# A column mean over 8192 rows: six 32 KB buffers used as a chain and then as a ring, instead of two pairs and a single

## Chip, core, metric

One core of one Trainium2 chip. The metric is the device time of one execution in microseconds; several executions are timed and medians quoted. The profile's span is about 2 us shorter than the time; where I take a time line apart, I use the span. Buffers are given per partition: 32 KB is one row group, 128 rows of 8192 fp32 values, 4.194 MB over all partitions.

## The reference

```python
def setup_inputs():
    return {"x": np.random.randn(8192, 8192).astype(np.float32)}

def reference(x):
    return np.mean(x, axis=0)
```

268.4 MB are read, and 32 KB are written.

## The kernel before

Row groups arrive by DMA. VectorE adds each into `acc`; at the end TensorE multiplies by a block of 1/8192 to sum over the partitions, with the last rows going to TensorE partly without a VectorE add. Five row groups of landing room (two pairs, one single) and `acc` make six buffers of 32 KB.

```python
pairs = [sb.tile([P, 2, N], f32, name=f"pair{i}") for i in range(2)]
single = sb.tile([P, N], f32, name="single")
acc = sb.tile([P, N], f32, name="acc")
...
def load(dst, src):
    queue = nc.sync if g < 30 else nc.scalar       # two DMA queues, one after the other
    queue.dma_start(out=dst, in_=src)
...
while g < G - 5:                                   # pair, pair, single, pair, pair, single ...
    if k % 3 < 2:
        t = pairs[i]
        load(t[:], rows(g, 2).rearrange("(p j) c -> p j c", j=2))
        ...                                        # the first pair makes acc
            add(t[:, 0, :], 0, N)                  # acc += first row group
            add(t[:, 1, :], 0, N)                  # acc += second row group
    else:
        load(single[:], rows(g))
        add(single, 0, N)
...
plan = [                                           # order of the closing matmuls, 512 columns each
    (r61, 0, 5), (r62, 8, 15), (acc, 8, 15), (r63, 0, 8), (acc, 0, 8), (acc, 15, 16),
    (r63, 8, 12), (r63, 12, 15), (r63, 15, 16),
]
...
# outputs: banks 0 and 1 on SyncE's queue, bank 2 and bank 3 on ScalarE's, edge on SyncE's
```

Of the kernel before, what the change touches and what calls it, by code (L numbers as in the profile page):

```python
# [1 line left out]

# [4 lines left out]


@with_exitstack
def kernel(  # L10
    ctx: ExitStack,
    tc: tile.TileContext,
    x: bass.AP,
    out: bass.AP,
):













    nc = tc.nc
    f32 = mybir.dt.float32  # L30
    M, N = x.shape
    P = nc.NUM_PARTITIONS
    F = 512
    W = F // 4
    NBLK = N // F - 1
    G = M // P

    sb = ctx.enter_context(tc.tile_pool(name="sb", bufs=1))
    psp = ctx.enter_context(tc.tile_pool(name="psum", bufs=1, space=bass.MemoryType.PSUM))

    pairs = [sb.tile([P, 2, N], f32, name=f"pair{i}") for i in range(2)]
    single = sb.tile([P, N], f32, name="single")
    acc = sb.tile([P, N], f32, name="acc")
    ones = sb.tile([P, 32], f32, name="ones")
    warm = sb.tile([P, 32], f32, name="warm")
    nc.gpsimd.memset(ones[:], 1.0 / M)  # L46
    nc.scalar.copy(out=warm[:], in_=ones[:])  # L47
    banks = [psp.tile([P, F], f32, name=f"bank{b}") for b in range(4)]
    edge = psp.tile([P, W], f32, name="edge")

    def add(row, lo, hi):
        nc.vector.tensor_add(out=acc[:, lo:hi], in0=acc[:, lo:hi], in1=row[:, lo:hi])  # L52

    def load(dst, src):
        queue = nc.sync if g < 30 else nc.scalar
        queue.dma_start(out=dst, in_=src)  # L56

    def rows(g, n=1):
        return x[g * P:(g + n) * P, :]

    g = 0
    k = 0
    np_ = 0
    while g < G - 5:
        if k % 3 < 2:
            i = np_ % 2
            np_ += 1
            t = pairs[i]
            load(t[:], rows(g, 2).rearrange("(p j) c -> p j c", j=2))
            if g == 0:  # L70
                nc.vector.tensor_add(out=acc[:], in0=t[:, 0, :], in1=t[:, 1, :])  # L71
            else:
                add(t[:, 0, :], 0, N)
                add(t[:, 1, :], 0, N)
            g += 2
        else:
            load(single[:], rows(g))
            add(single, 0, N)
            g += 1
        k += 1  # L80

    pa, pb = pairs[np_ % 2], pairs[(np_ + 1) % 2]
    r59, r60, r61, r62, r63 = single, pa[:, 0, :], pa[:, 1, :], pb[:, 0, :], pb[:, 1, :]
    load(r59[:], rows(g))
    add(r59, 0, N)
    load(r60, rows(g + 1))
    add(r60, 0, N)
    load(r61, rows(g + 2))
    add(r61, 5 * F, N)
    for lo, hi in [(0, 8), (8, 16)]:  # L90
        load(r62[:, lo * F:hi * F], rows(g + 3)[:, lo * F:hi * F])
    add(r62, 0, 8 * F)
    add(r62, NBLK * F, N)
    for lo, hi in [(0, 8), (8, 12), (12, 15), (15, 16)]:
        load(r63[:, lo * F:hi * F], rows(g + 4)[:, lo * F:hi * F])

    plan = [
        (r61, 0, 5),
        (r62, 8, 15),
        (acc, 8, 15),  # L100
        (r63, 0, 8),
        (acc, 0, 8),
        (acc, 15, 16),
        (r63, 8, 12),
        (r63, 12, 15),
        (r63, 15, 16),
    ]
    left = [sum(lo <= i < hi for _, lo, hi in plan) for i in range(NBLK + 1)]
    full = list(left)
    for row, lo, hi in plan:  # L110
        for i in range(lo, hi):
            for q in range(4) if i == NBLK else [i % 4]:
                c = i * F + (q * W if i == NBLK else 0)
                dst = edge if i == NBLK else banks[i // 4]
                tc.keep_in_program_order(nc.tensor.matmul(  # L115
                    out=dst[32 * q:32 * q + 32, :],
                    lhsT=ones[:],
                    rhs=row[:, c:c + (W if i == NBLK else F)],
                    start=left[i] == full[i],
                    stop=left[i] == 1,  # L120
                    tile_position=(0, 32 * q),
                    skip_group_check=True,
                ))
            left[i] -= 1

    res01 = sb.tile([P, 2, F], f32, name="res01")
    res2 = sb.tile([P, F], f32, name="res2")
    res3 = sb.tile([P, F], f32, name="res3")
    resedge = sb.tile([P, W], f32, name="resedge")
    nc.scalar.copy(out=res01[:, 0, :], in_=banks[0][:])  # L130
    nc.scalar.copy(out=res01[:, 1, :], in_=banks[1][:])  # L131
    nc.vector.tensor_copy(out=res2[:], in_=banks[2][:])  # L132
    tc.keep_in_program_order(nc.scalar.copy(out=res3[:96, :], in_=banks[3][:96, :]))  # L133
    nc.vector.tensor_copy(out=resedge[:], in_=edge[:])  # L134
    nc.sync.dma_start(
        out=out[0:8 * F].rearrange("(b q c) -> q b c", b=2, q=4), in_=res01[0:P:32, :, :])
    tc.keep_in_program_order(nc.scalar.dma_start(
        out=out[8 * F:12 * F].rearrange("(q c) -> q c", q=4), in_=res2[0:P:32, :]))
    tc.keep_in_program_order(nc.scalar.dma_start(
        out=out[12 * F:15 * F].rearrange("(q c) -> q c", q=3), in_=res3[0:96:32, :]))  # L140
    tc.keep_in_program_order(nc.sync.dma_start(
        out=out[15 * F:].rearrange("(q c) -> q c", q=4), in_=resedge[0:P:32, :]))


# [1 line left out]
_INS = ['x']  # L146
_OUTS = [((8192,), 'float32')]


# [23 lines left out]
```

## Time and profile before

| | before |
|---|---|
| time, median of 4 runs | 631.94 us (631.73 to 632.30) |
| span of the profiled run | 629.3 us |
| DMA engines, a full window | 433 GB/s, share 1.00 |
| VectorE | 533.6 us, 85% |
| last load landed (landing records of the trace) | 624.0 us |

The row to read first is that of the DMA engines, since it is full. The lines, and what follows from them, are in the prediction below.

### The profile page before, as it was taken

The page shows a single profiled execution, that of the slowest core. Times are in us where ns is not written, and L with a number is a line of the kernel's source. Part 1 is how long each engine was busy: PE and PEld are TensorE (multiplying, and loading weights), DVE is VectorE, ACT ScalarE, POOL GpSimd, SP SyncE. Part 2 cuts the span into 40 slices and gives each one's busy share as a digit, 9 for nine tenths or more (in the row PEclk, how much of TensorE's full clock was granted, in tenths as well). Part 3 has the DMA queues.
Part 4 walks back from the last instruction along what each step waited for, and adds up shares of the span by engine and source line. Part 5 has one row for each costly group of instructions (what it writes and reads, how often), then busy time and mean ns, then how long its engine had stood idle before and what let it go on. Part 6 is the DMA issues. An engine that isn't in the chain of part 4 may idle for free.

```text
span 629.3 us, 444 instructions
## 1 busy us (share of the span) xinstructions
PE 14.9 (2%) x100; PEld 4.9 (1%) x100; DVE 533.6 (85%) x65; ACT 3.3 (1%) x5; POOL 0.3 (0%) x5
## 2 busy tenths in 40 slices
PE   0000000000000000000000000000000000000027
PEld 0000000000000000000000000000000000000002
DVE  0539889889889889899499999888988988988995
ACT  0000000000000000000000000000000000000001
POOL 0000000000000000000000000000000000000000
PEclk9999999999999999999999999999999999999998
DMA  9999999999999999999999999999999999999995
GB/s 400 408 429 442 454 406 460 408 433 442 450 408 458 417 425 437 454 408 450 421 454 412 454 412 454 413 454 412 454 412 454 412 454 412 454 412 427 431 426 238
DMA packets 6371, 268.48 MB, mean 427 GB/s; under 512 B 719, under 2 KB 723, under 8 KB 994
## 3 DMA queue, kind: packets, MB, share of 16 engines
q10 hardware_dynamic: 3758, 142.62, 52.5%
q1 hardware_dynamic: 2612, 125.85, 46.3%
q14 instruction: 1, 0.01, 0.0%
HBM read 268.44 MB, written 0.03 MB: 427 GB/s over the span
## 4 chain that ended last, share of the span: by engine, by line
DMA 63%; DVE 35%; PE 2%; issue 0%; ACT 0%; SPq 0%; ACTq 0%; DVEq 0%
DMA pair<-in_x_dram 55%; DVE acc L52 35%; DMA single<-in_x_dram 8%; PE bank L115 2%; ACT res L133 0%; SPq L56 0%; PE edge L115 0%; ACTq L56 0%; DVEq L52 0%
## 5 line engine op out<-in xcount | busy, mean ns | idle before, releaser
L52 DVE TENSOR_TENSOR acc<-acc,pair 128x8192 f32<-128x8192 f32 (+3 forms) x50 | 419.6, 8393 | 56.5 <-DMA pair<-in_x_dram 55.5
L52 DVE TENSOR_TENSOR acc<-acc,single 128x8192 f32<-128x8192 f32 x12 | 104.3, 8692 | 9.4 <-DMA single<-in_x_dram 9.1
L71 DVE TENSOR_TENSOR acc<-pair 128x8192 f32<-128x8192 f32 x1 | 8.7, 8691 | 22.7 <-DMA pair<-in_x_dram 22.7
L115 PE MATMUL bank<-pair,ones 128*32 128x512 f32 x54 | 11.9, 800 | 610.7 <-DMA pair<-in_x_dram 610.7
L115 PEld LDWEIGHTS bank<-pair,ones 128*32 128x32 f32 x54 | 2.6, 128 | 616.4 <-issue 616.1
L115 PE MATMUL bank<-acc,ones 128*32 128x512 f32 x30 | 6.2, 661 | 0.0
L130 ACT COPY res<-bank 128x512 f32<-128x512 f32 x1 | 0.6, 587 | 620.3 <-DMA pair<-in_x_dram 620.3
L132 DVE COPY res<-bank 128x512 f32<-128x512 f32 x1 | 0.7, 692 | 3.2 <-PE bank L115 3.2
L115 PEld LDWEIGHTS bank<-acc,ones 128*32 128x32 f32 x30 | 1.7, 125 | 2.9 <-issue 2.5
L47 ACT ACT_TABLE_LOAD x1 | 1.3, 1283 | 0.7 <-PEq L157 0.7
L115 PE MATMUL edge<-pair,ones 128*32 128x128 f32 x8 | 0.8, 276 | 0.0
L115 PE MATMUL edge<-acc,ones 128*32 128x128 f32 x8 | 0.8, 272 | 0.0
L134 DVE COPY resedge<-edge 128x128 f32<-128x128 f32 x1 | 0.3, 291 | 0.4 <-PE bank L115 0.4
L133 ACT COPY res<-bank 96x512 f32<-96x512 f32 x1 | 0.6, 582 | 1.3 <-PE bank L115 1.3
L131 ACT COPY res<-bank 128x512 f32<-128x512 f32 x1 | 0.6, 586 | 0.3 <-PE bank L115 0.3
L115 PEld LDWEIGHTS edge<-acc,ones 128*32 128x32 f32 x8 | 0.5, 110 | 0.5 <-issue 0.3
L115 PEld LDWEIGHTS edge<-pair,ones 128*32 128x32 f32 x8 | 0.4, 109 | 0.6 <-issue 0.6
L47 ACT COPY warm<-ones 128x32 f32<-128x32 f32 x1 | 0.2, 217 | 0.0
L46 POOL MEMSET ones<- 128x32 f32 x1 | 0.1, 125 | 0.3 <-POOLq L157 0.3
L157 POOL MEMSET const-bfloat16-1.0<- 128x1 bf16 x1 | 0.1, 102 | 0.0
L157 POOL MEMSET const-uint8-127<- 128x1 uint8 x1 | 0.1, 102 | 0.0
L157 POOL MEMSET const-float32-0.0<- 128x1 f32 x1 | 0.1, 99 | 0.2 <-issue 0.2
(1 smaller groups left out, 0.1 us busy)
## 6 DMA issues: line engine op xcount, KB each, us to landing
single<-in_x_dram SPq DMA_DIRECT2D x6, 4096.0 KB, 40.3
single<-in_x_dram ACTq DMA_DIRECT2D x6, 4096.0 KB, 31.9
pair<-in_x_dram ACTq DMA_DIRECT2D x2, 4096.0 KB
pair<-in_x_dram ACTq DMA_DIRECT2D x3, 2048.0 KB, 26.3
pair<-in_x_dram ACTq DMA_DIRECT2D x1, 1024.0 KB, 28.4
pair<-in_x_dram ACTq DMA_DIRECT2D x1, 768.0 KB, 29.8
pair<-in_x_dram ACTq DMA_DIRECT2D x1, 256.0 KB, 29.9
pair<-in_x_dram SPq DMA_DIRECT2D x12, 30.9
```

The costliest lines, as they stand in the source:

```text
L46: nc.gpsimd.memset(ones[:], 1.0 / M)
L47: nc.scalar.copy(out=warm[:], in_=ones[:])
L52: nc.vector.tensor_add(out=acc[:, lo:hi], in0=acc[:, lo:hi], in1=row[:, lo:hi])
L71: nc.vector.tensor_add(out=acc[:], in0=t[:, 0, :], in1=t[:, 1, :])
L115: tc.keep_in_program_order(nc.tensor.matmul(out=dst[32 * q:32 * q + 32, :], lhsT=ones[:], rhs=row[:, c:c + (W if i == NBLK else F)], start ...
L130: nc.scalar.copy(out=res01[:, 0, :], in_=banks[0][:])
L131: nc.scalar.copy(out=res01[:, 1, :], in_=banks[1][:])
L132: nc.vector.tensor_copy(out=res2[:], in_=banks[2][:])
L133: tc.keep_in_program_order(nc.scalar.copy(out=res3[:96, :], in_=banks[3][:96, :]))
L134: nc.vector.tensor_copy(out=resedge[:], in_=edge[:])
L157: nc = _bacc.Bacc("TRN2", target_bir_lowering=False, num_devices=1)
```

## The change

It was meant to let nearly all loads be pairs, to halve the number of VectorE instructions in the opening, to have VectorE wait for one thing at a time, and to leave TensorE less to do after the last load, with fewer output transfers in each other's way. Cut to its core:

```diff
+    bufs = sb.tile([P, U, N], f32, name="bufs")     # U = 6
+    acc = bufs[:, U - 1, :]
-        queue = nc.sync if g < 30 else nc.scalar
+        queue = nc.sync if g < 30 and g != 2 else nc.scalar
+    def add(dst, src, dma=None, own=True):
+        ins = nc.vector.tensor_add(out=dst, in0=dst, in1=src).ins
+        ...
+        if dma and own:      # a GpSimd nop waits for load and previous add, VectorE for the nop
+        ...
+    while g < CHAIN:                                 # CHAIN = 12 row groups
+        u = g % U
+        dmas.append(load_pair(u, u + 1))
+        ...                                          # v: the pair of buffers before u
+            add(bufs[:, u:u + 2, :], bufs[:, v:v + 2, :], dmas[-1])   # 16384 columns
+        g += 2
+    add(acc, bufs[:, U - 2, :])
+    while g < G - 8:                                 # ring of five
+        dma = load_pair((g - CHAIN) % (U - 1), (g + 1 - CHAIN) % (U - 1))
+        add(buf(g + 1), buf(g), dma, own=False)
+        add(acc, buf(g + 1))
+        g += 2
+    ...                                              # five single rows, then r61, r62, r63
     plan = [
         (r61, 0, 5),
+        (acc, 8, 15),
         (r62, 8, 15),
-        (acc, 8, 15),
-        (r63, 0, 8),
         (acc, 0, 8),
         (acc, 15, 16),
+        (r63, 0, 8),
...
+    # outputs: banks 0 to 2 in one transfer, then bank 3, on SyncE's queue; edge on ScalarE's
```

More of the change, by code (lines that the diff above doesn't have):

```diff
@@ L36 @@
     G = M // P
+    U = 6
+    CHAIN = 12
+    sync = mybir.DependencyInfo(mybir.DependencyClass.Sync, mybir.DependencyReason.DATA)
     sb = ctx.enter_context(tc.tile_pool(name="sb", bufs=1))
     psp = ctx.enter_context(tc.tile_pool(name="psum", bufs=1, space=bass.MemoryType.PSUM))
-    pairs = [sb.tile([P, 2, N], f32, name=f"pair{i}") for i in range(2)]
-    single = sb.tile([P, N], f32, name="single")
-    acc = sb.tile([P, N], f32, name="acc")
+    bufs = sb.tile([P, U, N], f32, name="bufs")
+    acc = bufs[:, U - 1, :]
     ones = sb.tile([P, 32], f32, name="ones")
@@ L49 @@
     edge = psp.tile([P, W], f32, name="edge")
-    def add(row, lo, hi):
-        nc.vector.tensor_add(out=acc[:, lo:hi], in0=acc[:, lo:hi], in1=row[:, lo:hi])
     def load(dst, src):
-        queue = nc.sync if g < 30 else nc.scalar
-        queue.dma_start(out=dst, in_=src)
+        queue = nc.sync if g < 30 and g != 2 else nc.scalar
+        ins = queue.dma_start(out=dst, in_=src).ins
+        tc.add_to_no_dep_group("loads", ins)
+        return ins
     def rows(g, n=1):
         return x[g * P:(g + n) * P, :]
-    g = 0
@@ L62 @@
-    k = 0
-    np_ = 0
-    while g < G - 5:
-        if k % 3 < 2:
-            i = np_ % 2
-            np_ += 1
-            t = pairs[i]
-            load(t[:], rows(g, 2).rearrange("(p j) c -> p j c", j=2))
-            if g == 0:
-                nc.vector.tensor_add(out=acc[:], in0=t[:, 0, :], in1=t[:, 1, :])
-            else:
-                add(t[:, 0, :], 0, N)
-                add(t[:, 1, :], 0, N)
-            g += 2
-        else:
-            load(single[:], rows(g))
-            add(single, 0, N)
-            g += 1
-        k += 1
@@ L82, with load_pair @@
-    pa, pb = pairs[np_ % 2], pairs[(np_ + 1) % 2]
-    r59, r60, r61, r62, r63 = single, pa[:, 0, :], pa[:, 1, :], pb[:, 0, :], pb[:, 1, :]
-    load(r59[:], rows(g))
-    add(r59, 0, N)
-    load(r60, rows(g + 1))
-    add(r60, 0, N)
-    load(r61, rows(g + 2))
-    add(r61, 5 * F, N)
-    for lo, hi in [(0, 8), (8, 16)]:
-        load(r62[:, lo * F:hi * F], rows(g + 3)[:, lo * F:hi * F])
-    add(r62, 0, 8 * F)
-    add(r62, NBLK * F, N)
+    def load_pair(a, b):
+        a, b = sorted((a, b))
+        return load(bufs[:, a:b + 1:b - a, :], rows(g, 2).rearrange("(p j) c -> p j c", j=2))
@@ new lines @@
+    adds = []
+    def add(dst, src, dma=None, own=True):
+        ins = nc.vector.tensor_add(out=dst, in0=dst, in1=src).ins
+        dmas = dma if isinstance(dma, list) else [dma] if dma else []
+        if dma and own:
+            nop = tc.keep_in_program_order(nc.gpsimd.nop()).ins
+            for o in dmas + adds[-1:]:
+                tc.add_manual_dep(nop, o.name, sync, reason="GpSimd waits for it")
+            for group in ("loads", "adds"):
+                tc.declare_no_dep(ins, group=group, reason="GpSimd waited for it")
+            tc.add_manual_dep(ins, nop.name, sync, reason="waits for both at once")
+        elif dma:
+            tc.declare_no_dep(ins, group="loads", keep=dmas, reason="long landed")
+            tc.declare_no_dep(ins, group="adds", reason="the load waited for it")
+        tc.add_to_no_dep_group("adds", ins)
+        adds.append(ins)
@@ new lines, with buf @@
+    g = 0
+    dmas = []
+    while g < CHAIN:
+        u = g % U
+        dmas.append(load_pair(u, u + 1))
+        if g == 2:
+            add(bufs[:, u:u + 2, :], bufs[:, u - 2:u, :], dmas)
+        elif g:
+            v = (u - 2) % U
+            add(bufs[:, u:u + 2, :], bufs[:, v:v + 2, :], dmas[-1])
+        g += 2
+    add(acc, bufs[:, U - 2, :])
+    def buf(g):
+        return bufs[:, (g - CHAIN) % (U - 1), :]
+    while g < G - 8:
[3 more added lines that the diff above has]
+        g += 2
@@ L94 @@
+    while g < G - 3:
+        add(acc, buf(g), load(buf(g), rows(g)))
+        g += 1
+    r61, r62, r63 = [buf(g + j) for j in range(3)]
+    dma = load(r61, rows(g))
+    add(acc[:, 5 * F:], r61[:, 5 * F:], dma)
+    g += 1
+    dmas = [load(r62[:, lo * F:hi * F], rows(g)[:, lo * F:hi * F]) for lo, hi in [(0, 8), (8, 16)]]
+    add(acc[:, :8 * F], r62[:, :8 * F], dmas[0])
+    add(acc[:, NBLK * F:], r62[:, NBLK * F:], dmas[1])
+    g += 1
     for lo, hi in [(0, 8), (8, 12), (12, 15), (15, 16)]:
-        load(r63[:, lo * F:hi * F], rows(g + 4)[:, lo * F:hi * F])
+        load(r63[:, lo * F:hi * F], rows(g)[:, lo * F:hi * F])
@@ L124 @@
             left[i] -= 1
-    res01 = sb.tile([P, 2, F], f32, name="res01")
-    res2 = sb.tile([P, F], f32, name="res2")
+    res = sb.tile([P, 3, F], f32, name="res")
     res3 = sb.tile([P, F], f32, name="res3")
     resedge = sb.tile([P, W], f32, name="resedge")
-    nc.scalar.copy(out=res01[:, 0, :], in_=banks[0][:])
-    nc.scalar.copy(out=res01[:, 1, :], in_=banks[1][:])
-    nc.vector.tensor_copy(out=res2[:], in_=banks[2][:])
+    nc.scalar.copy(out=res[:, 0, :], in_=banks[0][:])
+    nc.scalar.copy(out=res[:, 1, :], in_=banks[1][:])
+    nc.vector.tensor_copy(out=res[:, 2, :], in_=banks[2][:])
     tc.keep_in_program_order(nc.scalar.copy(out=res3[:96, :], in_=banks[3][:96, :]))
@@ L135 @@
     nc.sync.dma_start(
-        out=out[0:8 * F].rearrange("(b q c) -> q b c", b=2, q=4), in_=res01[0:P:32, :, :])
+        out=out[0:12 * F].rearrange("(b q c) -> q b c", b=3, q=4), in_=res[0:P:32, :, :])
+    tc.keep_in_program_order(nc.sync.dma_start(
+        out=out[12 * F:15 * F].rearrange("(q c) -> q c", q=3), in_=res3[0:96:32, :]))
     tc.keep_in_program_order(nc.scalar.dma_start(
-        out=out[8 * F:12 * F].rearrange("(q c) -> q c", q=4), in_=res2[0:P:32, :]))
-    tc.keep_in_program_order(nc.scalar.dma_start(
-        out=out[12 * F:15 * F].rearrange("(q c) -> q c", q=3), in_=res3[0:96:32, :]))
-    tc.keep_in_program_order(nc.sync.dma_start(
         out=out[15 * F:].rearrange("(q c) -> q c", q=4), in_=resedge[0:P:32, :]))
```

## The prediction

> **What bounds the kernel now.** I read the page's slices first, to see whether any engine has room, then its DMA part, then windows of one buffer period each, and last the timeline of both ends.
>
> ```profile
> span 629.3 us, 444 instructions
> DVE  0539889889889889899499999888988988988995
> DMA  9999999999999999999999999999999999999995
> HBM read 268.44 MB, written 0.03 MB: 427 GB/s over the span
> ```
>
> The row of the DMA engines is full in every slice but the last, while VectorE (DVE), the next busiest, has gaps all along. The kernel reads 268.44 MB once, and cannot read less.
>
> ```profile
> 48.40:96.80 48.40, 0.00 (x0) 0.00 (x0) 43.45 (x6) 0.00 (x0) 0.00 (x0) 1.00 1.00 433
> 193.60:242.00 48.40, 0.00 (x0) 0.00 (x0) 43.45 (x6) 0.00 (x0) 0.00 (x0) 1.00 1.00 433
> 484.00:532.40 48.40, 0.00 (x0) 0.00 (x0) 43.45 (x6) 0.00 (x0) 0.00 (x0) 1.00 1.00 433
> ```
>
> These are windows of one period (pair, pair, single: five row groups of 4.194 MB). The fields are window, length, busy time of the five engines, clock, DMA share, GB/s. Each shows a DMA share of 1.00 and 433 GB/s, with VectorE busy 43.45 of 48.40 us. So 268.44 MB take 268.44/0.4333 = 619.5 us whatever the buffers are. What a change can touch is 629.3 - 619.5 = 9.8 us: the start, the end, and any hole that it opens in the stream.
>
> ```profile
> 0.74 0.86 SPq L56 DMA_DIRECT2D pair<-in_x_dram  x2
> 22.72 8.69 DVE L71 TENSOR_TENSOR acc<-pair 128x8192 f32<-128x8192 f32 x1 [22.72 <-DMA pair<-in_x_dram]
> 31.44 0.33 SPq L56 DMA_DIRECT2D pair<-in_x_dram  x1
> ...
> 623.17 0.29 PE L115 MATMUL edge<-acc,ones 128*32 128x128 f32 x3
> 623.39 1.47 PE L115 MATMUL bank<-pair,ones 128*32 128x512 f32 x10
> 625.11 0.40 PE L115 MATMUL edge<-pair,ones 128*32 128x128 f32 x6
> ...
> 625.89 0.56 SPq L141 DMA_DIRECT2D out_dram<-resedge  x1
> 626.63 0.73 ACTq L139 DMA_DIRECT2D out_dram<-res  x1
> ```
>
> These are rows of the timeline (start, length, what). The first pair is issued at 0.74 and used at 22.72, so **an issue into an idle stream lands 22.0 us later**, of which 8.39 MB at 433 GB/s are 19.4; some 2.6 us are latency at the two ends. At the end TensorE still works off `acc` columns (edge<-acc) at 623.2 to 623.6, although VectorE's last add was over by 621.3, and the last output is issued at 626.63, on the queue that had just spent 625.40 to 626.53 issuing another.
>
> **What the Trainium skill says.** "DMA: Bandwidth & Descriptors", section Specifications, gives a ceiling of 435 GB/s for the 16 engines on the SBUF side. The windows agree: 433 to 435. So the middle has no more than 0.5% left.
>
> The same page, section "Queues, rings and completion order", says that each DMA engine takes turns packet by packet between the queues that hold work for it. The trace agrees. At row group 30 the loads move from SyncE's queue to ScalarE's, and the single row group 29, issued on SyncE's at 261.94 and overtaken by a pair that ScalarE issued at 282.27, landed only at 310.6, 48.7 us after its issue, where the median single of that queue needs 40.3.
>
> "VectorE: DVE Perf Modes", section on the trn2 errata, gives (N+151)/0.96 ns for an fp32 two-tensor add. For 8192 columns that is 8691 ns, and the trace has 8692. So a chained add of 16384 columns should take 17.22 us (an estimate from that formula), against 17.42 for the two adds with their hand-over today.
>
> **The change part by part.**
>
> *Start of the stream.* Pair 0 goes on SyncE's queue, pair 1 on ScalarE's. By the turn-taking above they share, and both land at about 42.1 us, the time at which pair 1 is used today. The first chained add needs both, so VectorE starts at 42.1 and not at 22.7. This costs nothing by itself: the bytes flow.
>
> *Chain of two-row adds.* While one chained add runs, it holds four of the six buffers (source and target pair), so only one pair can be in flight. The next pair may be issued only when the add ends. The loop is: landing, 0.1 us for the hop over GpSimd (my guess; the present hand-over from landing to start is 0.07), 17.22 us of add, 0.03 to the issue (31.41 to 31.44 in the timeline), then 22.0 to landing, together 39.35 us for two pairs. The stream alone would need 2 x 19.37 = 38.74. So each of the five pairs issued after a chained add (row groups 6, 8, 10, 12, 14; two interleaved loops) lags by up to 0.3 us, the first by 0.6: **up to 1.8 us of holes**. The 22.0 was measured from a cold start. An engine still finishing its last packets when the new ones arrive hides part of this, so I take half: **+0.9 us**.
>
> *Ring of five.* In the steady ring the pair after next waits for the first 8.69 us add of the current pair, and the pair in flight lasts 19.37, so its issue comes some 10 us early. No hole and no gain: 433 GB/s as before. VectorE is busy 17.4 of 19.37 us, 90%, as now. The number of row groups that travel in 32 KB pieces is 14 in both (before: 12 singles and two of the tail; after: six singles and four pairs whose two buffers are not neighbours).
>
> *Queue change at row group 30.* Pair 28 waits on SyncE's queue when pair 30 is issued on ScalarE's 8.7 us after pair 26 landed. From then on the two share, and pair 28, which had some 9.2 us left, lands about 9.5 us late, at 28.5 us after pair 26. Pair 32 needs a buffer that the first add of pair 28 frees, at 28.5 + 8.7 = 37.2. Pair 30 ends at 38.7. Issue at 37.2 plus 22.0 is 59.2, against 58.1 for an unbroken stream: a hole of up to 1.1 us that the present buffers do not have (the window 278.30 to 302.50 is full today). With the same doubt about the 22.0 I take **+0.7 us**.
>
> *GpSimd's joined waits.* They are on VectorE's path, which has 10% to spare; outside the chain they cost and save nothing at the end.
>
> *The tail.* Seven single loads let VectorE finish `acc` earlier relative to the stream. Counting from the landing of pair 54: rows of 8.7 us from 17.4 on give row 60 done at 61.0, the partial adds at 67.0, 71.5 and 72.2 (6.0, 4.4 and 0.7 us, from the groups), while the last bytes land near 77.5. That is 5.3 us ahead; today 621.3 against about 624.0, 2.7. With the new order of matmuls all `acc` work precedes the last row, so after the last landing only eight edge matmuls remain: TensorE ends about 0.5 us sooner. The outputs go as one transfer of three banks, then one on each queue, so none waits behind 1.13 us of issuing on ScalarE's queue: the last issue moves from 626.63 to about 625.5. **-1.1 us**; the head start of `acc` is part of this sum.
>
> *Sum*, taking the 2.7 us between span and measured time as unchanged: 631.98 + 0.9 + 0.7 - 1.1 = **632.5 us**.
>
> **The rivals.**
>
> First, no holes at all: descriptors queue early enough that an engine never drains in the chain or at the queue change. For it: 2.6 us of latency are mostly overlapped whenever the queue is not empty, and the margin missed is only 0.6 us. Against it: each chained add ends only about 1.5 us before the pair in flight has all its bytes, and no issue in the present trace shows what so late a one costs. Then the tail alone counts: 630.9 us.
>
> Second, the holes are larger than the loop says: a drained stream restarts slowly, or the wait over GpSimd takes nearer 1 us, or the hole at the queue change repeats before the ring has caught up. Speaking for it is that six to seven loads are exposed; against it, that the ring regains 10 us of lead within a few pairs. With the full 1.8 and 1.1, and half a microsecond more per chained add from the hop, about 1.5 us in the interleaved loops: 635 us.
>
> Third, VectorE becomes the bound, because its start moves from 22.7 to 42.1 us and one more add (buffer 4 into `acc`) ends the chain. Against it: it works 17.4 per 19.37 us and gains 2 us on the stream with each pair, so a lag of 8.7 us is gone after five pairs. I expect no effect on the end.
>
> **Range and chances.** The two hole terms run from 0 to about 3 us and the tail from -0.5 to -1.5, so 8 times in 10 the time lies between 630.4 and 634.4. Faster by 2% would mean under 619.3, which is below the time of the bytes themselves. Slower by 2% needs 12.6 us of holes, four times what I count. So faster 0.01, same 0.98, slower 0.01.
>
> **What would show it.** In the profile of the changed kernel: 433 GB/s in every full period from 330 to 600 us; a DMA share below 1.00 in windows around 60 to 140 us, and once near 315; a VectorE wait of some 10 us at row group 28; chained adds of 17.22 us; a last output issue about 1.1 us closer to the last load's landing. A middle that runs above 435 GB/s or below 430 would make the prediction wrong from the ground, as would a GpSimd wait that shows as more than half a microsecond between a landing and its add.

## The result

| | before | changed |
|---|---|---|
| time, median of 4 runs | 631.94 us | 637.49 us (636.64 to 639.33) |
| span of the profiled run | 629.3 us | 635.6 us |
| last load landed | 624.0 us | 630.3 us |
| from there to the end of the span | 5.3 us | 5.3 us |

The ratio is 1.0091, with a 95% interval of 1.0069 to 1.0114. A ratio here is the mean time of one kernel's runs over that of the other's in the same rounds, so not quite the ratio of the medians quoted. By the 2% rule this is "same", as forecast; but the loss is clear of the noise, and 637.49 lies outside the predicted range of 630.4 to 634.4.

The page of the changed kernel, against the lines shown for before:

```profile
span 635.6 us, 404 instructions
DVE  0038978899999898887699988988889888899993
DMA  9999999999999999999999999999999999999995
HBM read 268.44 MB, written 0.03 MB: 422 GB/s over the span
```

In tenths, the DMA row still looks full: a slice of 16 us hides a hole of one. Windows of one pair (19.4 us) show it. First the kernel before, then the changed one (window, length, busy time of five engines, clock, DMA share, GB/s):

```profile
61.40:80.80 19.40, 0.00 (x0) 0.00 (x0) 16.45 (x3) 0.00 (x0) 0.00 (x0) 1.00 1.00 432
100.20:119.50 19.30, 0.00 (x0) 0.00 (x0) 16.43 (x2) 0.00 (x0) 0.00 (x0) 1.00 1.00 435
```

```profile
61.40:80.80 19.40, 0.00 (x0) 0.00 (x0) 17.23 (x1) 0.00 (x0) 0.00 (x0) 1.00 0.95 402
100.20:119.50 19.30, 0.00 (x0) 0.00 (x0) 17.19 (x2) 0.00 (x0) 0.00 (x0) 1.00 0.91 384
...
487.60:506.90 19.30, 0.00 (x0) 0.00 (x0) 17.33 (x3) 0.00 (x0) 0.00 (x0) 1.00 1.00 435
```

The DMA share falls to 0.95 and 0.91 in the chain and is whole again late in the ring. (A single window also counts packets at its edges, so the sum matters more than one share.) The timeline of the changed kernel shows why (start, length, what, idle time before it and what ended it):

```profile
42.29 17.23 DVE L75 TENSOR_TENSOR bufs<-bufs 128x16384 f32<-128x16384 f32 x1 [42.29 <-POOLq L78]
59.55 0.33 SPq L60 DMA_DIRECT2D bufs<-in_x_dram  x1
61.43 17.23 DVE L75 TENSOR_TENSOR bufs<-bufs 128x16384 f32<-128x16384 f32 x1 [1.91 <-POOLq L78]
78.69 0.33 SPq L60 DMA_DIRECT2D bufs<-in_x_dram  x1
84.06 17.23 DVE L75 TENSOR_TENSOR bufs<-bufs 128x16384 f32<-128x16384 f32 x1 [5.41 <-POOLq L78]
101.32 0.33 SPq L60 DMA_DIRECT2D bufs<-in_x_dram  x1
103.40 17.22 DVE L75 TENSOR_TENSOR bufs<-bufs 128x16384 f32<-128x16384 f32 x1 [2.11 <-POOLq L78]
...
123.21 17.23 DVE L75 TENSOR_TENSOR bufs<-bufs 128x16384 f32<-128x16384 f32 x1 [2.59 <-POOLq L78]
```

Each load on SyncE's queue (SPq) starts 0.03 us after a chained add ends: 42.29 + 17.23 = 59.52, then 59.55. The load issued at 59.55 is used at 84.06, 24.5 us later, and not 22.0 as the prediction had it from the cold start. VectorE then stands idle for 5.41 us. The release is put down to GpSimd (POOLq), but the load's landing record is at 84.00, 0.06 before the start: GpSimd only passed it on.

By the landing records it takes 121.5 us from when the first two pairs (row groups 0 to 3) have both landed to the landing of row groups 14 and 15. Six pairs at 433 GB/s need 6 x 19.37 = 116.2. So the chain lost 5.3 us. One more step, to row group 32 behind the queue change, took 20.6 instead of 19.4, 1.2 us. Together 6.5, against 6.3 between the two kernels' last landings; the 0.2 left over is within the scatter of single steps.

In the tail the two last outputs are issued sooner, and the end doesn't come sooner:

```profile
631.06 0.70 SPq L162 DMA_DIRECT2D out_dram<-res  x1
631.71 1.11 ACTq L166 DMA_DIRECT2D out_dram<-resedge  x1
631.87 0.79 SPq L164 DMA_DIRECT2D out_dram<-res  x1
```

```profile
SPq L193 <- DMA out_dram<-resedge: 0.7, 1, 0.7
```

The last issue is 1.6 us behind the last landing at 630.3, where before it was 2.6 (626.63 - 623.99). The second fence, SyncE's view of the waits, says that it then waited 0.7 us for the edge output (resedge) after the others were in. The packet records show what came in between: an 8 KB packet of the instruction queue, 0.58 us long, began at 632.9 among the output packets, and one 512 B packet of the edge output came only behind it, some 0.5 us after its three companions.

### The profile page after: what moved, and what is told of

Its sections match the earlier page's. It is cut to its first block, busy times and chain, and to the rows that moved or that the text cites. A ratio compares the mean times of both kernels' runs of the same rounds, so it can differ in the third digit from the quotient of the medians.

```text
span 635.6 us, 404 instructions
## 1 busy us (share of the span) xinstructions
PE 14.8 (2%) x100; PEld 4.4 (1%) x100; DVE 532.4 (84%) x60; ACT 3.3 (1%) x5; POOL 0.3 (0%) x5
## 4 chain that ended last, share of the span: by engine, by line
DMA 53%; DVE 45%; PE 2%; issue 0%; ACT 0%; POOLq 0%
DMA bufs<-in_x_dram 53%; DVE bufs L75 45%; PE bank L143 2%; ACT res L160 0%; POOLq L78 0%; PE edge L143 0%
## 5 line engine op out<-in xcount | busy, mean ns | idle before, releaser
L75 DVE TENSOR_TENSOR bufs<-bufs 128x8192 f32<-128x8192 f32 (+4 forms) x58 | 531.4, 9169 | 93.8 <-POOLq L78 54.3
L143 PE MATMUL bank<-bufs,ones 128*32 128x512 f32 x84 | 14.6, 753 | 616.5 <-DMA bufs<-in_x_dram 610.9
L143 PEld LDWEIGHTS bank<-bufs,ones 128*32 128x32 f32 x84 | 3.8, 128 | 625.6 <-issue 617.2
L143 PE MATMUL edge<-bufs,ones 128*32 128x128 f32 x16 | 1.6, 274 | 0.0
```

The lines of the kernel that those rows point to most:

```text
L75: ins = nc.vector.tensor_add(out=dst, in0=dst, in1=src).ins
L143: tc.keep_in_program_order(nc.tensor.matmul(out=dst[32 * q:32 * q + 32, :], lhsT=ones[:], rhs=row[:, c:c + (W if i == NBLK else F)], start ...
```

## The experiments

My theory: **late issue**. While a chained add runs, four of the six buffers are held, so the next load is issued about when the DMA engines run dry; the stream has holes, and their size is set by how the slowest of the 16 engines restarts. Rivals: **GpSimd's hop** delays the adds; **the chain costs once** (VectorE's late start, the wide adds, one more add at its end); **the queue** of the second pair or the queue change at row group 30; the **tail**. Times are medians; "before" is the old kernel in the same rounds, which moved between 631.1 and 631.9 from one set of rounds to the next, so ratios are what to compare.

| run | time, us | ratio to before (95%) | chain stretch, us |
|---|---|---|---|
| changed kernel again (e0) | 637.53 | 1.0101 (1.0080 to 1.0121) | 121.8 |
| ring from the start (e1) | 631.48 | 1.0001 (0.9984 to 1.0019) | 116.8 |
| no queue change (e2) | 637.50 | 1.0097 (1.0082 to 1.0112) | 123.0 |
| no GpSimd (e3) | 636.88 | 1.0088 (1.0072 to 1.0103) | 122.5 |
| ring, one queue (e4) | 631.19 | 0.9993 (0.9981 to 1.0006) | 116.3 |
| before + new tail (e5) | 632.95 | 1.0020 (1.0008 to 1.0033) | |
| chain, single loads (e6) | 631.19 | 0.9989 (0.9973 to 1.0004) | 116.2 |
| chain, split adds (e7) | 636.52 | 1.0073 (1.0059 to 1.0086) | 122.7 |
| first later issue (e8) | 637.18 | 1.0102 (1.0080 to 1.0123) | 121.5 |
| chain of 24 (e9) | 644.25 | 1.0207 (1.0189 to 1.0225) | 123.0 |
| chain of 6 (e10) | 632.63 | 1.0022 (1.0000 to 1.0045) | 118.9 |
| single loads, one queue (e11) | 631.01 | 0.9994 (0.9982 to 1.0007) | 116.2 |
| issue 1.76 us later (e12) | 637.91 | 1.0101 (1.0087 to 1.0115) | 122.8 |
| issue 0.69 us later (e13) | 638.21 | 1.0107 (1.0092 to 1.0123) | 121.3 |
| before + new outputs (e14) | 631.63 | 0.9999 (0.9986 to 1.0011) | |

The last column is the stretch just described, from the landing records: twelve row groups after the first two pairs; 116.2 is an unbroken stream.

### e0: the changed kernel again

No edit.

> The changed kernel once more, unaltered, for its spread and for the holes in its load stream. Late-issue theory (T1: a chained add holds four of six buffers, so the next pair is issued about when the DMA engines run dry, and the restart of the slowest of the 16 engines decides): 636.5 to 639.5 us, a spread many times that of the kernel before (0.6 us), and holes at the same pairs (row groups 6 and 14, where pairs were used 22.6 and 21.2 us after the one before, and 32) but of other sizes. GpSimd theory (T2: the joined waits delay the adds by a fixed hop): the same time within 0.3 us and the same holes.

The four runs lie between 636.82 and 638.14 us. The stretch of the chain lost 5.6 us again, but in other places: the first hole was 2.2 us and not 3.3, and the step to row group 32 was 19.4, no hole at all. The spread of this kernel was 1.3 us here and 2.7 in its first four runs. I had set it against the 0.6 us of the kernel before; but that kernel too spread over 1.9 us (630.54 to 632.41) in these rounds, so spread says nothing for the theory.

### e1: the ring from the first row group

```diff
-    CHAIN = 12
+    CHAIN = 0
-        queue = nc.sync if g < 30 and g != 2 else nc.scalar
+        queue = nc.sync if g < 30 else nc.scalar
-    add(acc, bufs[:, U - 2, :])
+        if g == 0:   # in the ring's loop
+            adds.append(nc.vector.tensor_add(out=acc, in0=buf(g), in1=buf(g + 1)).ins)
```

> No chain: the ring of five from the first row group, first two pairs both on SyncE's queue. T1: the chain's holes (landings of pairs 3, 5 and 7 late by 3.3, 0.5 and 1.8 us, 5.5 together) are gone, the hole at the queue change (1.2 us) stays: 637.5 - 5.5 = 632.0, within 0.8. T2 has no GpSimd hop here either in the middle of the kernel, so it expects the same drop; the run without GpSimd tells them apart. Third theory (T3: it is the tail that lost, or the rate of the loads itself): 637 still.

631.48 us, 6.0 under the changed kernel of the same rounds, and level with before. The chain was the loss. As this also moved the second pair's queue, it doesn't by itself clear that; e6 and e11 do, as they keep it.

### e2: no queue change at row group 30

```diff
-        queue = nc.sync if g < 30 and g != 2 else nc.scalar
+        queue = nc.sync if g != 2 else nc.scalar
```

> All loads but the second pair on SyncE's queue, so that nothing changes queue at row group 30. T1: VectorE's wait of 9.2 us at row group 28 and the hole behind it (pair of row group 32 used 20.6 instead of 19.4 us after the one before) are gone: 637.5 - 1.2 = 636.3, with the chain's own spread of about 1 us on it. If the queue change is harmless: 637.5.

VectorE's long wait there is gone. First the changed kernel's timeline, then this run's:

```profile
306.63 26.02 DVE L75 TENSOR_TENSOR bufs<-bufs 128x8192 f32<-128x8192 f32 x3 [9.19 <-DMA bufs<-in_x_dram]
```

```profile
300.72 17.42 DVE L75 TENSOR_TENSOR bufs<-bufs 128x8192 f32<-128x8192 f32 x2 [1.92 <-DMA bufs<-in_x_dram]
320.07 17.42 DVE L75 TENSOR_TENSOR bufs<-bufs 128x8192 f32<-128x8192 f32 x2 [1.94 <-DMA bufs<-in_x_dram]
```

The time did not move, 637.50 against 637.53. In this trace the chain lost 6.8 us, 1.2 more than in e0, and e0 had no hole at the queue change to save. The hole there is real but uneven. In the landing records of ten traces (the changed kernel's two, e1, e3, e6 to e9, e12 and e13; e10, whose ring comes to it with other buffers, has no hole) the step to row group 32 is between 0.0 and 1.2 us longer than 19.37, 0.5 on average. That is less than the chain's own scatter (a stretch of 121.5 to 123.0 in the changed kernel, e0, e2 and e3), so e2 could not show it. The expected 1.2 us was a miss.

### e3: no GpSimd

```diff
-        if dma and own:
+        if dma and own and False:
...
-        elif dma:
+        elif dma and not own:
```

> The chain and the ring as in the change, but each add waits by itself for its load and for the add before, without GpSimd. T1: 637.5 within the spread of 1.5 us, the same holes. T2: 5 us less, 632.5, and VectorE's idle time before the chained adds falls.

```profile
83.30 17.22 DVE L75 TENSOR_TENSOR bufs<-bufs 128x16384 f32<-128x16384 f32 x1 [4.54 <-DMA bufs<-in_x_dram]
...
125.43 17.22 DVE L75 TENSOR_TENSOR bufs<-bufs 128x16384 f32<-128x16384 f32 x1 [5.30 <-DMA bufs<-in_x_dram]
```

In this run's timeline the chained adds wait as long as before, now with the DMA itself named. From landing to add it is 0.10 us there (83.20 to 83.30), where the hop over GpSimd took 0.06. 636.88 us: GpSimd's hop is not the cause. The 0.65 us gained is within the chain's scatter; this trace's tail was 0.9 us shorter than e0's (4.2 us from last landing to end against 5.1), with no instruction fetch among the output packets.

### e6 and e7: the chain with an earlier issue, and its control

Both cut each chained add in two of one row group and leave out GpSimd (with it, the split form did not pass a race check), so e3 is their base. e6 also cuts the chain's loads from row group 6 on:

```diff
-        dmas.append(load_pair(u, u + 1))
+        if g < U:
+            dmas.append(load_pair(u, u + 1))
+        else:
+            dmas.append([load(bufs[:, u + j, :], rows(g + j)) for j in range(2)])
...
-            add(bufs[:, u:u + 2, :], bufs[:, v:v + 2, :], dmas[-1])
+            add(bufs[:, u, :], bufs[:, v, :], one[0])          # e7: dmas[-1]
+            add(bufs[:, u + 1, :], bufs[:, v + 1, :], one[1])  # where cut; e7: no load
```

> The chain kept, but each chained add cut into two of one row group, and from row group 6 on the chain's loads cut likewise, so that the first half is issued 8.6 us earlier, some 10 us before the stream would run dry. No GpSimd waits, so the run without GpSimd is its base (636.9). T1: the chain's holes vanish, 631 to 632. If the chain costs by something else (VectorE's later start, the wide adds, the extra add at its end): 636 to 637 still.

> Control for the run before it: the chained adds cut in two, the loads left as pairs. A pair still waits for both buffers, so its issue comes 0.2 us later than in the base. T1: 636.5 to 638, holes as before. If the wide adds themselves were at fault: 631 to 632.

e6 took 631.19 us, e7 636.52 in the same rounds. The windows of e6, where the changed kernel had 0.95 and 0.91:

```profile
61.40:80.80 19.40, 0.00 (x0) 0.00 (x0) 19.39 (x3) 0.00 (x0) 0.00 (x0) 1.00 1.00 432
100.20:119.50 19.30, 0.00 (x0) 0.00 (x0) 19.30 (x3) 0.00 (x0) 0.00 (x0) 1.00 1.07 462
```

With the chain kept, VectorE started as late (42.16) and the second pair still on ScalarE's queue, an issue 8.6 us earlier took the whole loss away. It is the time of the issue that counts, and neither the chain as such nor that queue. (e6 also loads in pieces of one row group. That this form by itself is the cure was not tested, but e1 loads pairs, issues them 10.6 us or more before the load ahead has landed in this stretch, and loses next to nothing either: 116.8.)

### e9 and e10: more and fewer exposed loads

```diff
-    CHAIN = 12
+    CHAIN = 24      # e9;  e10: CHAIN = 6
```

> The chain over 24 row groups and not 12: eleven loads are issued after a chained add and not five. Late-issue theory: at 1.1 to 1.35 us for each exposed load (5.4 to 6.8 us for five in the traces of four runs with the chain), 6.6 to 8.1 us more: 644 to 646. If the chain costs once (the later start of VectorE, the extra add at its end): 637.5.

> The chain over the first six row groups: two exposed loads (row groups 6 and 8). Late-issue theory: 1.1 to 1.35 us each, of which the first hole alone had 2.2 to 3.3: 633.5 to 635. If the chain costs once: 637.5.

644.25 us with eleven exposed loads and 632.63 with two, where five gave 637.5. The loss grows with their number: from five to eleven 6.7 us, 1.1 each. e10 came out 0.9 us lower than the low end I had named; its stretch lost 2.7 us (118.9 - 116.2), nearly all at the first hole.

### e8, e12 and e13: an issue later still

The loop of the prediction said 0.3 us per exposed load, and the runs say 1.1 to 1.35. Is lateness simply larger, and paid again for each further microsecond, or is something special about loads that come just as an engine runs dry? e8 was to delay the issue by one more VectorE instruction that reads the buffers about to be reloaded:

```diff
+        if g:
+            old = bufs[:, (u - 2) % U, :1536]
+            nc.vector.tensor_add(out=scratch[:], in0=old, in1=old)
```

> The changed kernel with one more VectorE instruction after each chained add that reads 1536 columns of the buffer pair about to be reloaded, so that each exposed load is issued 1.76 us later (estimate from (1536+151)/0.96 ns). If lateness adds up simply, each of the three steps of the loop (row groups 6, 10, 14) loses 1.76 more: 637.5 + 5.3 = 642.8. If the loss at present is already the loss of a dry stream plus an irregular restart of engines that have only just run dry, a stream that is fully dry restarts evenly in 21.9 us from issue to landing and the loop is 17.35 + 1.76 + 21.9 = 41.0 for two pairs: from row group 2 to 14 it takes 123.0 us, against 121.6 to 123.0 in the traces so far, so about 638 to 639.

It failed as a test. The scheduler put the new instruction ahead of the chained add, so only the first two loads came later (61.08 and 80.01 instead of 59.5 and 78.6). Those two landed at 83.1 and 102.4, as in e0 (82.9 and 102.8), which was a hint. e12 and e13 read what the chained add wrote, which forces the order:

```diff
-            nc.vector.tensor_add(out=scratch[:], in0=old, in1=old)
+            nc.vector.tensor_add(out=scratch[:], in0=bufs[:, u, :1536], in1=old)   # e13: 512 columns
```

> As e8, but the extra instruction reads what the chained add wrote, so it must run after it: all five exposed loads are issued 1.76 us later. Simple lateness: three loop steps of 1.76, 637.5 + 5.3 = 642.8, and 127 to 128 us from the landing of row group 2 to that of 14. Dry stream that restarts evenly (issue to landing 21.9): 3 x 41.0 = 123.0 us for that stretch, and 638 to 639 us.

> The same with 512 columns, 0.69 us later (estimate from (512+151)/0.96 ns). Simple lateness: 637.5 + 2.1 = 639.6. Even restart once dry: 3 x 39.9 = 119.8 us for the stretch if the restart were even at this lateness too, but not below the 121.6 of the unchanged kernel if it is still uneven; 636 to 638 us.

The timeline of e12:

```profile
59.48 1.76 DVE L103 TENSOR_TENSOR scratch<-bufs 128x1536 f32<-128x1536 f32 x1
61.27 0.33 SPq L61 DMA_DIRECT2D bufs<-in_x_dram  x1
...
83.14 17.23 DVE L76 TENSOR_TENSOR bufs<-bufs 128x16384 f32<-128x16384 f32 x1 [2.77 <-POOLq L79]
```

Issued 1.72 us later than in the changed kernel, the load was used 0.92 us *earlier* (and about as early as in e0, 82.9). By the records, the five exposed loads of e12 took 21.81, 21.99, 21.78, 21.81 and 21.88 us from issue to landing (the first, third and fifth came to dry engines). In the changed kernel they took 24.46, 24.65, 21.83, 21.85 and 23.23 (the second also stood in line behind the first). The packet records of the first hole: in the changed kernel the 16 engines were done with the load before between 0.81 and 1.45 us after the new load's issue, and they began on it between 0.98 and 3.20 us after the issue. In e12 all 16 had been done at least 0.34 us before the issue, and they began between 0.96 and 1.87. (The records don't name a packet's engine, so which engines began last can't be read.)

So 1.76 us of added lateness in each of five loads cost nothing measurable (ratio 1.0101, as in e0), where simple lateness on top of the loss expected 5.3 us. e13, 0.69 us later, also stayed level (1.0107), its 638.21 us just above the range named. Its first two loads took 21.8 and 22.0 us and its later ones 22.5 to 22.9, in between; before its first hole the engines were done 0.26 to 0.70 us after the issue. The loop of the prediction, taken three times with 21.9 us from issue to landing, gives 117.8 us for the stretch of the changed kernel, 119.8 for e13 and 123.0 for e12. Measured were 121.5 to 123.0 (the first trace, e0, e2, e3), 121.3 and 122.8. So the loop is right for engines that have been dry for more than a microsecond when new work comes (e12, one run), and 3.7 to 5.2 us too short where it comes just as they run dry. What happens in an engine at that moment, no run here shows.

### e5 and e14: the tail on the old kernel

e5 gives the kernel before the new plan and the new outputs; e14 the new outputs alone.

> The kernel before with the new order of matmuls and the new output transfers, nothing else. If these are worth what the run without GpSimd and the run with the ring show between last landing and end (4.2 and 4.4 us, against 5.3 before): 1.0 us faster than before. If an instruction fetch falls between the output packets, as in the two traces of the changed kernel (8 KB, 0.4 to 0.6 us, behind which one 512 B packet of the edge output waits): no gain, 0.0.

> The kernel before with the new output transfers only, its order of matmuls kept. If the order of matmuls is what cost e5 its 1.1 us (its first output was issued 2.9 us after the last landing, against 0.05 in the kernel before): this run is 0 to 1.0 us faster than before. If the output transfers cost it: 1 us slower again.

e5 lost 0.2%, an outcome I had not named; e14 was level. So the outputs by themselves gain nothing measurable there, and by difference (no run has it alone) the new order of matmuls costs the old kernel about 1.2 us. The timeline of e5:

```profile
621.62 1.68 PE L115 MATMUL bank<-acc,ones 128*32 128x512 f32 x12
...
623.77 3.17 PE L115 MATMUL bank<-pair,ones 128*32 128x512 f32 x26
...
627.35 0.70 SPq L134 DMA_DIRECT2D out_dram<-res  x1
```

The program fixes the order of the matmuls, and `acc` work now stands ahead of row 63. With the old loads the last add into `acc` ends near 621.7, so the matmuls of row 63, whose first half had landed at 619.5, all come after 623.6, and the first output leaves at 627.35 instead of 624.03. TensorE also begins this part later, at 616.68 and not 614.25, and its clock record goes from half to full 4.3 us before the last landing, where before it was 5.6. The new order needs the head start that the single rows at the changed kernel's end give `acc`.

### e4 and e11: a version to beat both

e4 is e1 with all loads on SyncE's queue, e11 is e6 with all but the second pair there.

> Ring from the first row group and all loads on SyncE's queue: no exposed issue is left in the stream, with the new tail. Late-issue theory (T1): as the run with the ring alone, less what the queue change still costs (0 to 1.2 us): 0.0 to 1.0 us under the kernel before of the same rounds. If the middle hides another loss: equal to before or slower.

> The candidate: the chain with single-row loads, which had no hole, and all loads but the second pair on SyncE's queue. No hole is left and the new tail stays: 0.3 to 1.5 us under the kernel before of the same rounds, depending on where an instruction fetch and the half-clock stretch of TensorE fall in the tail.

631.19 and 631.01 us, ratios 0.9993 and 0.9994: level with the kernel before. Both beat the changed kernel by 6 us, and neither can be told from the old one. By medians e4 is 0.65 us under before (0.0 to 1.0 was expected) and e11 0.32 (0.3 to 1.5), but both intervals take in no gain at all.

## Why the prediction was wrong

- **The bound** was right: 433 to 435 GB/s in full windows, the bytes need 619.5 us, and neither kernel nor any experiment ran below it. "Within 2%" followed from that and held.
- **The chain's mechanism** was right: four of six buffers held, an issue 0.03 us after the add, chained adds of 17.22 to 17.23 us, a hop over GpSimd of 0.06 to 0.1 us.
- **The chain's size failed**, at the step "An engine still finishing its last packets when the new ones arrive hides part of this, so I take half: +0.9". I took the cold start's 22.0 us as the most an issue could need. Measured were 24.5 in the changed kernel's first hole; the term is 5.3 us, three times even my upper bound of 1.8. Loads that came just as the engines ran dry took up to 24.5 us, those that came to engines long dry 21.8 to 21.9 (e12): the partial overlap I counted as help was the harm.
- **The queue change**: the mechanism was right (VectorE's wait of 9.2 us at row group 28, then up to 1.2 us of hole against "up to 1.1"), and +0.7 is near the 0.5 that ten traces average, though e2 gained nothing by removing it. There is luck in it: in the first trace pair 28 landed 26.6 us after pair 26 and not 28.5, so that pair 32 was issued at 35.4 and not 37.2, but it then took 24.0 us and not 22.0.
- **The tail**: -1.1 was expected, 0.0 came, though the last issue did move by 1.05 us against the last landing. Over the traces with the new loads and the new tail, the stretch from last landing to end runs from 4.1 to 5.4 us (before: 5.3). Where the first output left within 0.4 us of the last landing (e1, e3, e6, e7, e9) it is 4.1 to 4.4, the gain that was expected. At 0.4 to 0.5 us (e8, e11, e12) it is 4.3 to 4.6. Where it left later, 0.8 to 1.3 us, as in the changed kernel, it is 5.1 to 5.4: TensorE was behind there. In the changed kernel its matmuls of 512 columns took 1.06 us each while the granted clock was 0.50, until 6.0 us before the last landing, and 0.59 at full clock. In e1 the short ones begin 7.2 us before the last landing and the first output leaves 0.2 us after it; in e10 it is 5.0 before and 1.3 after. (The windows view gives e1 a clock of 1.00 before that too, but its clock records only begin there; the matmuls of 1.06 us tell.) Three of these traces, the changed kernel's two and e2, also have the fetch among the outputs. So the gain was there, but it goes with where a stretch of half clock falls, which I had left out; how much of the loss is the fetch stays open, since e4 has a tail of 5.3 us without one.
- **The rivals**: the second, "a drained stream restarts slowly", named the right culprit with a time, 635 us, still too low. The GpSimd wait in it is refuted (e3), and so is the third, VectorE as the bound (e6).
- **Readings**: the "median single" of 40.3 us, a figure of the page, is a median of the four landings that the page could assign (31.9, 31.9, 48.6 and 50.1); by the landing records the other two took 31.9 us as well, so row group 29 was later still against the usual than I wrote. And six loads at the end are whole single rows, not seven.

In the sum, +0.9 should have been +5.3, and -1.1 should have been 0.0; with the queue term left as it was, that makes 631.98 + 5.3 + 0.7 + 0.0 = 638.0, against 637.5.

## What to carry to other kernels

When a stream of loads is the bound, work out for every load how long before the queue runs dry it can be issued, and count the buffers that a running instruction holds, source and target both. In the first hole the issue came 0.8 to 1.5 us before the engines ran dry, 1.8 us before the load ahead had landed; exposed loads lost 1.1 us each on average. How early is early enough can be read from the landing records of the ten traces with a chain of pairs (the changed kernel, e0, e2, e3, e7 to e10, e12, e13; fourth to thirteenth load). Loads issued 2.5 to 5.3 us before the load ahead had landed lost anything from nothing to 2.4 us, nine issued 5.6 to 7.3 us before it at most 0.25, and the 36 issued earlier still at most 0.15. So don't count on the last microseconds to overlap: free a buffer earlier, here by smaller adds and loads, which gave all 5 to 6 us back. A full-looking DMA row does not show holes of 1%; windows of one transfer's length do.

## What the Trainium skill lacked or had wrong

- "DMA: Bandwidth & Descriptors", section "Latency and other measured facts", gives about 600 ns to a HWDGE transfer's first byte. For the earliest engine the runs agree (in e12 the first packet began 0.96 us after the issue began and 0.63 after it ended), but the page has nothing on the other engines or on a restart: the last of the 16 began at 1.87 us when all were long dry, and at 3.20 us when the load came just as they ran dry (whole loads: 21.8 us against up to 24.5).
- The same page, section "Queues, rings and completion order", has queue row 14, the runtime's own, on the same 16 engines as a kernel's rows. It doesn't say what one of its packets costs a kernel: in three traces an 8 KB packet of 0.42 to 0.58 us fell among the output packets, and one packet of the edge output began 0.3 to 0.5 us behind its companions.
- "HBM Reference", section "Specifications (TRN2)", puts a core that streams alone at about 425 GB/s. Full windows here ran at 433 GB/s.
